# First projection group of a hybrid encoder layer: the weights' low parts on GpSimd, their products over two token blocks, a shorter norm

## The chip, the cores and the metric

The kernel runs on one core of a Trainium2 chip. The metric is the device time of one execution in microseconds (us). A core has five engines that run beside each other, each through its own instructions in order: PE (TensorE, matrix products and transposes into PSUM), DVE (VectorE) and ACT (ScalarE), which read PSUM and SBUF, POOL (GpSimd), which here works on SBUF alone, and SP, which issues DMA transfers. They wait for each other through semaphores.

## The reference

One layer: an RMSNorm of the input, one wide projection whose columns feed two token mixers (a chunkwise matrix memory and a stick-breaking attention) and two gates, a projection of each mixer, a gated sum, an output projection and the residual. Cut to what the change touches:

```python
D_MODEL = 1024; SEQ = 512; EPS = 1e-6

def rmsnorm(x, w):
    xf = x.astype(jnp.float32)
    y = xf * lax.rsqrt(jnp.mean(xf * xf, axis=-1, keepdims=True) + EPS)
    return (y * w.astype(jnp.float32)).astype(x.dtype)

h = rmsnorm(x, norm_w)
proj = jnp.einsum('bsd,de->bse', h, w_in) + b_in      # w_in: 1024 x 11272
```

The first group that the kernel computes is 512 columns of `w_in`: the queries of the first four attention heads, for all 512 tokens.

## The kernel before

**Products in three parts.** [...] A product is three matmuls into one PSUM bank: high by high, low by high, high by low. For weights the high part is a copy by ACT (`AF.Copy`) and the low part a subtraction by DVE (`split`, L96 to L98).

**The normalised input.** The 512 tokens are four blocks (tb) of 128. For a block, `x_scale` (L277) squares and sums the rows on ACT, makes the row's factor r = (mean + eps)^-0.5 with two small POOL instructions (`rstd`, L273: a scalar multiply-add and a power) and multiplies the rows by it on DVE (L290). The first block comes in two halves, with one POOL addition more (L286). `x_turn` (L292) then transposes the block on PE in two groups of four 128x128 pieces, into PSUM; DVE multiplies by the norm's weights `nw_t` and writes the high parts `hh` of a group (L302, one instruction) and its low parts `hl` (L306, four). `nw_t` itself is a PE transpose of the weights' rows and a DVE copy (L231, L232).

**The first group.** The program works through units in a hand-written order (the loop at L1226): at unit c it evacuates unit c - 1, prepares later weights, and issues the products of unit c in two halves. The first four units are the four token blocks of the first group, and each wants all eight k pieces (128 rows each) of that group's weights. So the weights of all four units (two k pieces each; L1141 to L1145 load them, the fourth into a buffer named P5) are split ahead of the loop: `first_split` (L1132) writes high parts `fh` on ACT and low parts `fl` on DVE for units 0 and 2, on POOL for units 1 and 3. `first_mm` (L1172) runs per k piece the three products in a row, into the bank `f_ps[tb]`: L1179 (hh by fh), L1180 (hl by fh), L1181 (hh by fl). A unit has two halves of four k pieces; `x_turn(c + 1)` stands between the halves of units 0 and 1, `x_turn(3)` behind unit 1. `x_scale(1)` is ahead of the loop, `x_scale(2)` and `x_scale(3)` are behind the first half of unit 0 and its `x_turn(1)`. Each engine's order is the order in which the code issues to it; no scheduler moves anything. Ahead of all this PE runs 11 matmuls on zeros (`warm`, L1155).

**Evacuation.** Unit c - 1's bank is read by DVE (L347, `qraw`) at the start of unit c. Four PSUM banks (`dps`) serve the dense products. Later weights arrive in three buffers `stg`, which units 0 to 2 hold first.

Of the kernel before, what the change touches and what calls it, by code (L numbers as in the profile page):

```python
# [8 lines left out]
F32 = mybir.dt.float32  # L9
FR = mybir.dt.float32r  # L10
BF = mybir.dt.bfloat16
AF = mybir.ActivationFunctionType
OP = mybir.AluOpType

D = 1024
T = 512
KT = 8
TB = 4
NQK = 18
EPS = 1e-6  # L20
# [15 lines left out]
def tile_hybrid_layer(  # L36
# [16 lines left out]
    nc = tc.nc  # L53
# [21 lines left out]
    def blk(tag, dt=F32, shape=(512,), name=None, p=128):  # L75

        where = mp if tag in MISC else sp
        return where.tile([p] + list(shape), dt, name=name or tag, tag=tag, bufs=BUFS[tag])

    def two(tag, dt=F32, name=None):  # L80

        t = blk(tag, dt, (2, 512), name=name)
        return t[:, 0, :], t[:, 1, :]

    def dense_ps():
        return psd.tile([128, 512], F32, name="dps", tag="dps")

    def att_ps():
        return psa.tile([128, 512], F32, name="aps", tag="aps")
# [40 lines left out]
    units = []  # L130
# [59 lines left out]
    def h_sta(k, tb):  # L190
        ts = slice(tb * 128, (tb + 1) * 128)
        return hh[:, k, ts], hl[:, k, ts]
# [27 lines left out]
    mhalf = cst.tile([128, 8], F32, name="mhalf")  # L220
# [6 lines left out]
    nw_t = cst.tile([128, 8], F32, name="nw_t")  # L227

    def norm_vec():
        vp = att_ps()  # L230
        nc.tensor.transpose(vp[:, 0:8], v_rows[0:8, :], ident[0:8, 0:8])  # L231
        nc.vector.tensor_copy(nw_t, vp[:, 0:8])  # L232

    def load_vecs():
        for j in range(4):
# [37 lines left out]
    def rstd(dst, ssq, n, eps):  # L273
        nc.gpsimd.tensor_scalar(dst, ssq, 1.0 / n, eps, op0=OP.mult, op1=OP.add)
        nc.gpsimd.tensor_tensor(dst, dst, mhalf[:, 0:dst.shape[1]], op=OP.pow)

    def x_scale(tb):  # L277
        xs = tiny.tile([128, 4], F32, name="xs", bufs=2)
        ssq, r = xs[:, 0:2], xs[:, 2:3]
        xn = x_t[tb]  # L280
        junk = blk("om", BF, (D,), name="junk")
        if tb == 0:
            for i in range(2):
                c = slice(i * D // 2, (i + 1) * D // 2)
                nc.scalar.activation(junk[:, c], xn[:, c], AF.Square, accum_out=ssq[:, i:i + 1])
            nc.gpsimd.tensor_tensor(ssq[:, 0:1], ssq[:, 0:1], ssq[:, 1:2], op=OP.add)  # L286
        else:
            nc.scalar.activation(junk, xn, AF.Square, accum_out=ssq[:, 0:1])
        rstd(r, ssq[:, 0:1], D, EPS)
        nc.vector.tensor_scalar(xn, xn, r, None, op0=OP.mult)  # L290

    def x_turn(tb):  # L292
        ts = slice(tb * 128, (tb + 1) * 128)
        xn = x_t[tb]
        for g in range(2):
            ks = slice(4 * g, 4 * g + 4)
            tp = att_ps()
            for j in range(4):
                kt = g * 4 + j
                nc.tensor.transpose(tp[:, j * 128:(j + 1) * 128], xn[:, kt * 128:(kt + 1) * 128], ident)  # L300
            dh = hh[:, ks, ts]
            nc.vector.tensor_tensor(dh, tp.rearrange("p (k t) -> p k t", k=4),  # L302
                                    nw_t[:, ks].unsqueeze(2).to_broadcast([128, 4, 128]), op=OP.mult)
            for j in range(4):
                k = 4 * g + j
                nc.vector.scalar_tensor_tensor(hl[:, k, ts], tp[:, j * 128:(j + 1) * 128], nw_t[:, k:k + 1],  # L306
                                               hh[:, k, ts].bitcast(F32), op0=OP.mult, op1=OP.subtract)
# [245 lines left out]
    def gates_fill():  # L553
        wg = blk("P5", FR, (KT, 128), name="wg")
        nc.gpsimd.memset(wg.bitcast(F32), 0.0)
        wg_t.append(wg)
# [505 lines left out]
    u = []  # L1062
# [66 lines left out]

    f_w = []  # L1130

    def first_split(i, low=None):  # L1132
        u = units[i]
        his = two("qk", FR, name="fh")
        for j in range(2):
            hi, lo = his[j], blk("y", FR, name="fl")
            nc.scalar.activation(hi, u.st[:, j, :], AF.Copy)
            (low or nc.vector).tensor_tensor(lo, u.st[:, j, :], hi.bitcast(F32), op=OP.subtract)
            f_w.append((hi, lo))

    units[0].load()  # L1141
    units[1].load()
# [12 lines left out]
    def warm(n):  # L1155
        for _ in range(n):
            nc.tensor.matmul(wp, idle[:, 0:128], idle, start=True, stop=True)

    warm(9)
    norm_vec()  # L1160
    x_scale(0)
    warm(2)
    first_split(0)
    x_turn(0)
    first_split(1, nc.gpsimd)
    x_scale(1)
    first_split(2)
    first_split(3, nc.gpsimd)

    f_ps = []  # L1170

    def first_mm(tb):  # L1172
        def mm(half):
            if half == 0:
                f_ps.append(dense_ps())
            for k in range(4 * half, 4 * half + 4):
                sh, sl = h_sta(k, tb)
                wh, wl = f_w[k]
                nc.tensor.matmul(f_ps[tb], sh, wh, start=k == 0, stop=False)  # L1179
                nc.tensor.matmul(f_ps[tb], sl, wh, start=False, stop=False)  # L1180
                nc.tensor.matmul(f_ps[tb], sh, wl, start=False, stop=k == KT - 1)  # L1181
        return mm

    for tb in range(TB):
        units[tb].mm = first_mm(tb)

    later.setdefault(3, []).append(turn_vecs)
    later.setdefault(GATES_PREP, []).append(gates_prep)
# [30 lines left out]
    def ahead(c):  # L1219
        while count["ready"] < min(N, c + AHEAD + 1):  # L1220
            fetch(count["ready"] + 1)
            units[count["ready"]].split()
            count["ready"] += 1
        fetch(c + LOADS + 1)

    for c in range(N):  # L1226
        now[0] = c
        if 0 < c < TB:
            ahead(c)
        if c and units[c - 1].slow:  # L1230
            units[c - 1].slow()
            ahead(c)
        due = later.pop(c, [])
        if c > n_proj - 9:
            ahead(c)
        if c:
            units[c - 1].evac()
        for fn in due:
            fn()
        ahead(c)  # L1240
        units[c].mm(0)
        if c < 2:
            x_turn(c + 1)
        if c == 0:
            x_scale(2)
            x_scale(3)
            gates_fill()
        for g in list(act):
            if c in REST:
                continue  # L1250
            if next(g, "end") == "end":
                act.remove(g)
        for e in list(pend):
            if c >= e[0] and e[2]():
                pend.remove(e)
                g = e[3]()
                next(g)
                act.append(g)
        units[c].mm(1)
        if c == 1:  # L1260
            x_turn(3)
# [31 lines left out]
```

## Time and profile before

| | |
|---|---|
| three runs | 692.78, 693.33, 693.89 us; median 693.33 us |
| profiled execution | 692.25 us, its span from first to last instruction 690.5 us |
| outside the span | 1.75 us |
| DVE busy | 466.4 us (68%) |
| ACT busy | 337.2 us (49%) |
| POOL busy | 118.1 us (17%) |
| granted TensorE clock, mean | 0.999 |

Of the page, the row of busy time tells which engine has no room; the view of waits tells how long an engine stood and for what; the timeline, cut to the first 32 us, gives start and length of each instruction of the first group. In a timeline row the first number is the start in us from the span's begin, the second the length, `x2` says that two instructions are merged, and what stands in brackets is idle time before it and what ended it. A PE matmul of 512 columns is shown with a length of 0.39 us, but follows its neighbour 0.23 us after that one's start.

### The profile page before, as it was taken

How to read it: one execution, taken by the hardware profiler on the slowest of the kernel's cores; microseconds unless marked ns; L12 is line 12 of the kernel's file. 1: busy time of each engine (PE TensorE's matmuls, PEld its weight loads, DVE VectorE, ACT ScalarE, POOL GpSimd, SP SyncE). 2: the span in 40 equal slices, each digit the busy share in tenths (PEclk: the TensorE clock that was granted, in tenths of full speed). 3: DMA queues.
4: the chain of work that ended last, by engine and by line, in shares of the span. 5: the costliest groups of instructions: out<-in, count | busy, mean ns of one | idle time of the engine just before them, and what ended most of it. 6: DMA issues, size and time to landing. Idle time of an engine off the chain costs nothing.

```text
span 690.5 us, 9365 instructions
## 1 busy us (share of the span) xinstructions
PE 681.7 (99%) x3150; PEld 568.2 (82%) x3150; DVE 466.4 (68%) x815; ACT 337.2 (49%) x631; POOL 118.1 (17%) x270
## 2 busy tenths in 40 slices
PE   7999999999999999999999999999999999999997
PEld 5888888888888888888888888888888888888885
DVE  6845787777997886789834648994352364445995
ACT  6235374565554653244466433447554343344451
POOL 5222032365430310000011210001112000111021
PEclk9999999999999999999999999999999999999999
DMA  7423544535553533553341343434223465599344
GB/s 249 138 92 109 155 117 121 144 89 152 146 157 102 130 106 85 124 109 92 106 110 59 106 103 90 127 89 135 71 64 90 114 189 189 140 210 207 108 90 124
DMA packets 122577, 85.27 MB, mean 123 GB/s; under 512 B 19050, under 2 KB 105988, under 8 KB 122528
## 3 DMA queue, kind: packets, MB, share of 16 engines
q1 hardware_dynamic: 119600, 77.97, 40.0%
q0 software_dynamic: 2784, 6.56, 5.1%
q8 instruction: 25, 0.41, 0.2%
q14 instruction: 24, 0.20, 0.1%
q10 hardware_dynamic: 144, 0.13, 0.1%
HBM read 66.22 MB, written 2.15 MB: 99 GB/s over the span
## 4 chain that ended last, share of the span: by engine, by line
PE 88%; issue 6%; DMA 3%; POOL 1%; DVE 1%; ACT 0%; SPq 0%; DVEq 0%; POOLq 0%
PE dps L92 25%; PE dps L93 25%; PE dps L94 25%; PE aps L93 2%; PE aps L94 2%; PE aps L92 2%; DMA xr<-in_x_dram 1%; PE dps L1181 1%; PE dps L1179 1%; PE dps L1180 1%; DMA xr<-u 1%; DMA stg<-in_w_in_dram 1%; PE aps L794 1%; PE aps L796 1%; PE aps L795 1%
## 5 line engine op out<-in xcount | busy, mean ns | idle before, releaser
L98 DVE TENSOR_TENSOR wl<-stg,wh 128x1024 fp32r<-128x1024 f32 x92 | 112.5, 1223 | 107.8 <-ACT wh L97 107.5
L92 PE MATMUL dps<-hh,wh 128*128 128x512 f32 x448 | 175.0, 391 | 0.0
L94 PE MATMUL dps<-hh,wl 128*128 128x512 f32 x448 | 174.4, 389 | 0.0
L93 PE MATMUL dps<-hl,wh 128*128 128x512 f32 x448 | 174.4, 389 | 0.0
L97 ACT ACTIVATE wh<-stg 128x1024 fp32r<-128x1024 f32 x92 | 96.8, 1052 | 65.3 <-PE dps L94 45.1
L94 PEld LDWEIGHTS dps<-hh,wl 128*128 128x128 f32 x448 | 84.1, 188 | 17.7
L93 PEld LDWEIGHTS dps<-hl,wh 128*128 128x128 f32 x448 | 84.1, 188 | 16.8
L92 PEld LDWEIGHTS dps<-hh,wh 128*128 128x128 f32 x448 | 84.2, 188 | 16.7
L92 PE MATMUL dps<-wh,hh 128*128 128x512 f32 x224 | 87.7, 392 | 0.0
L94 PE MATMUL dps<-wh,hl 128*128 128x512 f32 x224 | 87.3, 390 | 0.0
L93 PE MATMUL dps<-wl,hh 128*128 128x512 f32 x224 | 87.2, 389 | 0.0
L94 PEld LDWEIGHTS dps<-wh,hl 128*128 128x128 f32 x224 | 42.0, 188 | 9.0
L92 PEld LDWEIGHTS dps<-wh,hh 128*128 128x128 f32 x224 | 42.1, 188 | 8.3
L93 PEld LDWEIGHTS dps<-wl,hh 128*128 128x128 f32 x224 | 42.1, 188 | 8.2
L687 DVE SCALAR_TENSOR_TENSOR acc<-tmp,vec,acc 128x511 f32<-128x511 f32 (+2 forms) x48 | 36.0, 750 | 1.7
L690 ACT ACTIVATE tmp<-acc 128x512 f32<-128x512 f32 x16 | 10.1, 633 | 50.8 <-DVE acc L687 50.8
L463 POOL TENSOR_SCALAR_AFFINE_SELECT om<-om 128x128 f32<-128x128 f32 x32 | 15.4, 480 | 96.2 <-ACT om L461 96.1
L747 POOL TENSOR_SCALAR_AFFINE_SELECT w_all<-om 128x128 f32<-128x128 f32 x16 | 6.9, 465 | 142.1 <-DMA om<-rb_d 142.1
L469 DVE TENSOR_TENSOR_SCAN om<-om 128x512 f32<-128x512 f32 (+3 forms) x32 | 26.7, 834 | 5.5 <-POOL om L463 5.5
L461 ACT ACTIVATE om<-aps,rq 128x512 f32<-128x512 f32 (+3 forms) x32 | 16.8, 525 | 20.9 <-PE aps L94 20.9
L92 PE MATMUL dps<-yh,wh 128*128 128x512 f32 x64 | 24.9, 389 | 0.0
L93 PE MATMUL dps<-yl,wh 128*128 128x512 f32 x64 | 24.9, 389 | 0.0
(249 smaller groups left out, 1218.5 us busy)
## 6 DMA issues: line engine op xcount, KB each, us to landing
stg<-in_w_in_dram SPq DMA_DIRECT2D x87, 512.0 KB, 3.9
az<-ay SPq DMA_DIRECT2D x128, 40.0 KB, 2.8
stg<-in_w_proj_s_dram SPq DMA_DIRECT2D x8, 512.0 KB, 4.1
B<-in_w_out_dram SPq DMA_DIRECT2D x8, 512.0 KB, 5.8
stg<-in_w_proj_m_dram SPq DMA_DIRECT2D x8, 512.0 KB, 5.7
wl<-stg POOLq DMA_DIRECT2D x8, 512.0 KB, 5.8
tz<-ty SPq DMA_DIRECT2D x72, 32.0 KB, 1.9
brow<-in_b_in_dram SPq DMA_DIRECT2D x8, 256.0 KB, 4.4
```

The costliest lines, as they stand in the source:

```text
L92: nc.tensor.matmul(ps, ah, bh, start=first, stop=False)
L93: nc.tensor.matmul(ps, ah, bl, start=False, stop=False)
L94: nc.tensor.matmul(ps, al, bh, start=False, stop=last)
L97: nc.scalar.activation(hi, src, AF.Copy)
L98: nc.vector.tensor_tensor(lo, src, hi.bitcast(F32), op=OP.subtract)
L461: nc.scalar.activation(om[:, 0:n], zp, AF.Sigmoid, scale=rn[:, h:h + 1])
L463: nc.gpsimd.affine_select(out=om[:, ts], in_=om[:, ts], compare_op=OP.is_gt, fill=1.0, base=0, channel_multiplier=1, pattern=[[-1, 128]])
L469: nc.vector.tensor_tensor_scan(back, back, back, 1.0, op0=OP.mult, op1=OP.bypass)
L687: nc.vector.scalar_tensor_tensor(acc[:, j:], t[:, 0:T - j], cw(3 - j, ch), acc[:, j:], op0=OP.mult, op1=OP.add)
L690: nc.scalar.activation(t, acc, AF.Sigmoid)
L794: nc.tensor.matmul(nm[:, 0:258], ph, vh, start=j == 0, stop=False)
L795: nc.tensor.matmul(sum_v, ph, vl, start=False, stop=False)
```

## The change

It does four things, all ahead of or within the first four units.

1. The low parts `fl` of all eight k pieces are made by POOL, in pieces placed around the norm steps (`first_lo`); ACT's copies stay where they were.
2. Units 0 and 1 are run in another order. The products with `fl` stand behind main products (`first_main`: hh by fh, hl by fh) of later k pieces, those of k 4 to 7 of block 0 behind all main products of block 1. Two banks are then open at once, and both are evacuated at the start of unit 2. Units 2 and 3 keep their order.
3. The norm has one instruction less for the first block: r is the power -0.5 of (sum + sum + D*eps), the factor sqrt(D) goes into `nw_t`. For the other blocks POOL clears the second sum first, one instruction more.
4. `x_scale(2)` stands ahead of the loop, ahead of the last two `fl`.

```diff
-        nc.vector.tensor_copy(nw_t, vp[:, 0:8])
+        nc.vector.tensor_scalar(nw_t, vp[:, 0:8], D ** 0.5, None, op0=OP.mult)
...
-            nc.gpsimd.tensor_tensor(ssq[:, 0:1], ssq[:, 0:1], ssq[:, 1:2], op=OP.add)
         else:
+            nc.gpsimd.memset(ssq[:, 1:2], 0.0)
             nc.scalar.activation(junk, xn, AF.Square, accum_out=ssq[:, 0:1])
-        rstd(r, ssq[:, 0:1], D, EPS)
+
+        nc.gpsimd.tensor_scalar(r, ssq[:, 0:1], ssq[:, 1:2], D * EPS, op0=OP.add, op1=OP.add)
+        nc.gpsimd.tensor_tensor(r, r, mhalf[:, 0:1], op=OP.pow)
         nc.vector.tensor_scalar(xn, xn, r, None, op0=OP.mult)
...
+    def first_hi(i):
         his = two("qk", FR, name="fh")
         for j in range(2):
-            hi, lo = his[j], blk("y", FR, name="fl")
-            nc.scalar.activation(hi, u.st[:, j, :], AF.Copy)
-            (low or nc.vector).tensor_tensor(lo, u.st[:, j, :], hi.bitcast(F32), op=OP.subtract)
-            f_w.append((hi, lo))
+            nc.scalar.activation(his[j], units[i].st[:, j, :], AF.Copy)
+            f_w.append((his[j], blk("y", FR, name="fl")))
+
+    def first_lo(*ks):
+
+        for k in ks:
+            hi, lo = f_w[k]
+            nc.gpsimd.tensor_tensor(lo, units[k // 2].st[:, k % 2, :], hi.bitcast(F32), op=OP.subtract)
...
-    first_split(0)
+    first_hi(0)
     x_turn(0)
-    first_split(1, nc.gpsimd)
+    first_lo(0, 1)
+    first_hi(1)
+    first_lo(2)
     x_scale(1)
-    first_split(2)
-    first_split(3, nc.gpsimd)
+    first_lo(3)
+    first_hi(2)
+    first_hi(3)
+    first_lo(4, 5)
+    x_scale(2)
+    first_lo(6, 7)
...
+    def first_main(tb, ks):
+
+        if ks[0] == 0:
+            f_ps.append(dense_ps())
+        for k in ks:
+            sh, sl = h_sta(k, tb)
+            nc.tensor.matmul(f_ps[tb], sh, f_w[k][0], start=k == 0, stop=False)
+            nc.tensor.matmul(f_ps[tb], sl, f_w[k][0], start=False, stop=False)
+
+    def first_rest(tb, ks):
+        for k in ks:
+            nc.tensor.matmul(f_ps[tb], h_sta(k, tb)[0], f_w[k][1], start=False, stop=k == KT - 1)
...
+            if tb == 0 and half == 0:
+                first_main(0, range(4))
+                first_rest(0, range(2))
+                first_main(0, range(4, 6))
+            elif tb == 0:
+                first_rest(0, range(2, 4))
+                first_main(0, range(6, 8))
+            elif tb == 1 and half == 0:
+                first_main(1, range(8))
+            elif tb == 1:
+                first_rest(0, range(4, 8))
+                first_rest(1, range(8))
...
+    first_evacs = [units[0].evac, units[1].evac]
+    units[0].evac = lambda: None
+    units[1].evac = lambda: [fn() for fn in first_evacs]
...
         if c == 0:
-            x_scale(2)
             x_scale(3)
```

How it moves instructions is seen in each engine's order. First POOL, from the first block's norm on, before: `xs` holds a block's sums and its r (157 is block 0, 201 block 1, 258 block 2), `fl_195` and `fl_198` are the low parts of k 2 and 3, `fl_215` and `fl_218` those of k 6 and 7.

```order
L286 TENSOR_TENSOR xs_157<-xs_157 128x1
L274 TENSOR_SCALAR xs_157<-xs_157 128x1
L275 TENSOR_TENSOR xs_157<-xs_157,mhalf_91 128x1
L1138 TENSOR_TENSOR fl_195<-stg_115,fh_194 128x512
L1138 TENSOR_TENSOR fl_198<-stg_115,fh_194 128x512
L274 TENSOR_SCALAR xs_201<-xs_201 128x1
L275 TENSOR_TENSOR xs_201<-xs_201,mhalf_91 128x1
L1138 TENSOR_TENSOR fl_215<-P5_121,fh_214 128x512
L1138 TENSOR_TENSOR fl_218<-P5_121,fh_214 128x512
L274 TENSOR_SCALAR xs_258<-xs_258 128x1
L275 TENSOR_TENSOR xs_258<-xs_258,mhalf_91 128x1
```

The same engine and place of the changed kernel, behind the first block's norm: `xs_199` is now block 1, `xs_219` block 2, and `fl_168`, `170`, `195`, `197`, `209`, `211` are k 0 to 5.

```order
L1144 TENSOR_TENSOR fl_168<-stg_113,fh_166 128x512
L1144 TENSOR_TENSOR fl_170<-stg_113,fh_166 128x512
L1144 TENSOR_TENSOR fl_195<-stg_115,fh_193 128x512
L287 MEMSET xs_199 128x1
L290 TENSOR_SCALAR xs_199<-xs_199 128x1
L291 TENSOR_TENSOR xs_199<-xs_199,mhalf_91 128x1
L1144 TENSOR_TENSOR fl_197<-stg_115,fh_193 128x512
L1144 TENSOR_TENSOR fl_209<-stg_119,fh_207 128x512
L1144 TENSOR_TENSOR fl_211<-stg_119,fh_207 128x512
L287 MEMSET xs_219 128x1
L290 TENSOR_SCALAR xs_219<-xs_219 128x1
L291 TENSOR_TENSOR xs_219<-xs_219,mhalf_91 128x1
```

Block 1's factor stands behind three low parts where it stood behind two, block 2's behind six where it stood behind four. DVE before, from the scaling of block 0 (`x_80`) to the first high parts of block 1 (from `aps_238`); `x_117` is block 1:

```order
L290 TENSOR_SCALAR x_80<-x_80,xs_157 128x1024
L1138 TENSOR_TENSOR fl_168<-stg_113,fh_167 128x512
L1138 TENSOR_TENSOR fl_171<-stg_113,fh_167 128x512
L302 TENSOR_TENSOR hh_98<-aps_174,nw_t_97 128x4x128
L306 SCALAR_TENSOR_TENSOR hl_99<-aps_174,nw_t_97,hh_98 128x128 x4
L302 TENSOR_TENSOR hh_98<-aps_184,nw_t_97 128x4x128
L306 SCALAR_TENSOR_TENSOR hl_99<-aps_184,nw_t_97,hh_98 128x128 x4
L290 TENSOR_SCALAR x_117<-x_117,xs_201 128x1024
L1138 TENSOR_TENSOR fl_208<-stg_119,fh_207 128x512
L1138 TENSOR_TENSOR fl_211<-stg_119,fh_207 128x512
L302 TENSOR_TENSOR hh_98<-aps_238,nw_t_97 128x4x128
```

DVE of the changed kernel, the same place; `x_123` is block 2, and `aps_247` holds the transposes of block 1:

```order
L292 TENSOR_SCALAR x_80<-x_80,xs_157 128x1024
L304 TENSOR_TENSOR hh_98<-aps_171,nw_t_97 128x4x128
L308 SCALAR_TENSOR_TENSOR hl_99<-aps_171,nw_t_97,hh_98 128x128 x4
L304 TENSOR_TENSOR hh_98<-aps_181,nw_t_97 128x4x128
L308 SCALAR_TENSOR_TENSOR hl_99<-aps_181,nw_t_97,hh_98 128x128 x4
L292 TENSOR_SCALAR x_117<-x_117,xs_199 128x1024
L292 TENSOR_SCALAR x_123<-x_123,xs_219 128x1024
L304 TENSOR_TENSOR hh_98<-aps_247,nw_t_97 128x4x128
```

The four subtractions are gone, and the scaling of block 2 now stands ahead of block 1's high parts, where it stood behind them. PE of the changed kernel from the end of unit 0's first half to the first product of unit 1 (`dps_284`; unit 0's bank is `dps_232`); `fh_207` is k 4 and 5, `fh_212` k 6 and 7:

```order
L1190 MATMUL dps_232<-fh_207,hl_99 128x512
L302 MATMUL aps_247<-ident_86,x_117 128x128 x4
L302 MATMUL aps_257<-ident_86,x_117 128x128 x4
L1194 MATMUL dps_232<-fl_195,hh_98 128x512
L1194 MATMUL dps_232<-fl_197,hh_98 128x512
L1189 MATMUL dps_232<-fh_212,hh_98 128x512
L1190 MATMUL dps_232<-fh_212,hl_99 128x512
L1189 MATMUL dps_232<-fh_212,hh_98 128x512
L1190 MATMUL dps_232<-fh_212,hl_99 128x512
L1189 MATMUL dps_284<-fh_166,hh_98 128x512
```

Behind block 1's transposes stand 6 matmuls of unit 0, where 12 stood, and the first product of unit 1, which takes block 1's high parts, comes next.

More of the change, by code (lines that the diff above doesn't have):

```diff
@@ L1130, in tile_hybrid_layer @@
     f_w = []
-    def first_split(i, low=None):
-        u = units[i]
+    def first_hi(i):
         his = two("qk", FR, name="fh")
         for j in range(2):
-            hi, lo = his[j], blk("y", FR, name="fl")
-            nc.scalar.activation(hi, u.st[:, j, :], AF.Copy)
-            (low or nc.vector).tensor_tensor(lo, u.st[:, j, :], hi.bitcast(F32), op=OP.subtract)
-            f_w.append((hi, lo))
+            nc.scalar.activation(his[j], units[i].st[:, j, :], AF.Copy)
[4 more added lines that the diff above has]
+            nc.gpsimd.tensor_tensor(lo, units[k // 2].st[:, k % 2, :], hi.bitcast(F32), op=OP.subtract)
     units[0].load()
@@ L1162, in tile_hybrid_layer @@
     warm(2)
-    first_split(0)
+    first_hi(0)
     x_turn(0)
-    first_split(1, nc.gpsimd)
+    first_lo(0, 1)
+    first_hi(1)
+    first_lo(2)
     x_scale(1)
-    first_split(2)
-    first_split(3, nc.gpsimd)
-    f_ps = []
+    first_lo(3)
[4 more added lines that the diff above has]
+    first_lo(6, 7)
+    f_ps = []
+    def first_main(tb, ks):
[8 more added lines that the diff above has]
+            nc.tensor.matmul(f_ps[tb], h_sta(k, tb)[0], f_w[k][1], start=False, stop=k == KT - 1)
     def first_mm(tb):
         def mm(half):
[L1174 to L1181, printed above, removed]
+            if tb == 0 and half == 0:
[10 more added lines that the diff above has]
+                first_rest(1, range(8))
+            else:
+                for k in range(4 * half, 4 * half + 4):
+                    first_main(tb, [k])
+                    first_rest(tb, [k])
         return mm
```

## The prediction

> **What bounds the kernel now.** I read the page's busy row first, then what PE waits for, then whether anything behind the first group gives PE a pause, then the first 32 us in order of time.
>
> ```profile
> PE 681.7 (99%) x3150; PEld 568.2 (82%) x3150; DVE 466.4 (68%) x815; ACT 337.2 (49%) x631; POOL 118.1 (17%) x270
> PE dps L1157 <- DVE idle L1152: 1.5, 1, 1.5
> PE dps L1179 <- ACT fh L1137: 1.3, 1, 1.3
> PE aps L300 <- DVE x L290: 0.8, 1, 0.8
> PE dps L1181 <- DVE fl L1138: 0.7, 1, 0.7
> PE   7999999999999999999999999999999999999997
> ```
>
> PE is the bound. The four waits are all that the view lists for it (total, times, longest), and the last row, the span in 40 slices with PE's busy share in tenths, places them: only the first slice, 17 us long, and the last fall short of 9. The change leaves the number of matmuls as it is. So its worth is read from one instant: **when PE starts the first product of unit 2**, from where on both programs run the same products. A shift there goes through to the end.
>
> ```profile
> 6.96 1.10 PE L300 MATMUL aps<-ident,x 128*128 128x128 f32 x8
> 9.40 0.47 PE L1179 MATMUL dps<-fh,hh 128*128 128x512 f32 x1 [1.34 <-ACT fh L1137]
> 9.70 0.49 PE L1180 MATMUL dps<-fh,hl 128*128 128x512 f32 x1
> 10.03 0.39 PE L1181 MATMUL dps<-fl,hh 128*128 128x512 f32 x1
> ...
> 20.87 0.39 PE L1181 MATMUL dps<-fl,hh 128*128 128x512 f32 x1
> 21.10 1.03 PE L300 MATMUL aps<-ident,x 128*128 128x128 f32 x8
> 21.89 0.48 PE L1179 MATMUL dps<-fh,hh 128*128 128x512 f32 x1
> 22.21 0.40 PE L1180 MATMUL dps<-fh,hl 128*128 128x512 f32 x1
> ...
> 25.51 0.48 PE L1179 MATMUL dps<-fh,hh 128*128 128x512 f32 x1
> ```
>
> Unit 2 starts at **25.51**. A matmul follows the one before after 0.23 us (20.87 to 21.10), the first behind a block's transposes takes 0.32 (21.89 to 22.21), and the eight transposes take 0.79 (21.10 to 21.89).
>
> **What the change takes away.** The norm of block 0 first.
>
> ```profile
> 4.94 0.19 POOL L286 TENSOR_TENSOR xs<-xs 128x1 f32<-128x1 f32 x1 [3.49 <-ACT junk L285]
> 5.22 0.19 POOL L274 TENSOR_SCALAR xs<-xs 128x1 f32<-128x1 f32 x1
> 5.49 0.56 POOL L275 TENSOR_TENSOR xs<-xs,mhalf 128x1 f32<-128x1 f32 x1
> 5.96 0.17 DVE L232 COPY nw_t<-aps 128x8 f32<-128x8 f32 x1 [4.50 <-PE aps L231]
> 6.15 0.76 DVE L290 TENSOR_SCALAR x<-x,xs 128x1024 f32<-128x1024 f32 x1
> ```
>
> One step of 0.28 us (4.94 to 5.22) goes, so r is there at 5.78 in place of 6.05. But DVE, in order, makes `nw_t` ahead of the scaling, until 6.13, and that waits for PE. The scaling stays at 6.15: worth **0**. The multiply that replaces the copy, 8 columns wide, is costed as the copy's 0.17; at most it takes the 0.76 of a multiply over 1024 columns, 0.6 more, which the wait found below would hide.
>
> Without the two subtractions DVE reaches block 0's high parts earlier.
>
> ```profile
> 7.35 1.29 DVE L1138 TENSOR_TENSOR fl<-stg,fh 128x512 fp32r<-128x512 f32 x2 [0.45 <-ACT fh L1137]
> 8.56 0.69 DVE L302 TENSOR_TENSOR hh<-aps,nw_t 128x512 fp32r<-128x512 f32 x1
> ```
>
> Half of block 0's eight transposes (6.96, 1.10 for all) are done near 7.6, so `hh` starts at 7.65 in place of 8.56 and PE's first product at about 8.5 in place of 9.40. That 0.9 us counts only if nothing stops PE later.
>
> **What it adds: POOL's queue.** Block 1's and block 2's factors now stand behind three and six low parts.
>
> ```profile
> 6.69 1.15 ACT L1137 ACTIVATE fh<-stg 128x512 fp32r<-128x512 f32 x2 [1.83 <-DMA stg<-in_w_in_dram]
> 8.23 1.15 ACT L1137 ACTIVATE fh<-stg 128x512 fp32r<-128x512 f32 x2 [0.39 <-DMA stg<-in_w_in_dram]
> 10.72 1.16 ACT L1137 ACTIVATE fh<-stg 128x512 fp32r<-128x512 f32 x2
> 13.36 1.06 ACT L288 ACTIVATE junk<-x 128x1024 bf16<-128x1024 f32 x1 [0.21 <-DMA x<-in_x_dram]
> 8.93 1.29 POOL L1138 TENSOR_TENSOR fl<-stg,fh 128x512 fp32r<-128x512 f32 x1 [2.88 <-ACT fh L1137]
> 10.18 1.29 POOL L1138 TENSOR_TENSOR fl<-stg,fh 128x512 fp32r<-128x512 f32 x1
> 11.55 0.19 POOL L274 TENSOR_SCALAR xs<-xs 128x1 f32<-128x1 f32 x1
> 11.83 0.56 POOL L275 TENSOR_TENSOR xs<-xs,mhalf 128x1 f32<-128x1 f32 x1
> L462 POOL MEMSET om<- 128x1 f32 x32 | 3.1, 96 | 0.0
> ```
>
> ACT's order does not change. POOL's k 2 started 0.70 behind the start of ACT's copy (8.23 to 8.93), so k 0 starts at 6.69 + 0.70 = 7.39. A low part takes 1.29 us, and the next starts 1.25 behind it (8.93 to 10.18). Three end at 7.39 + 2.50 + 1.29 = 11.18. A clear (0.1), the addition and the power (from the start at 11.55 to 12.39: 0.84, with 0.08 ahead) bring **r of block 1 at 12.19**, where it was 12.39: a gain of 0.2 us, no more. ACT's k 4 and k 5, 0.7 and 1.3 us behind 10.72, are there before POOL wants them.
>
> Then come the low parts of k 3, 4 and 5. At 1.25 each from 12.14 they end at 15.93, and with the same 1.05 us **r of block 2 comes at 16.98 at the earliest**. The squares of block 2 (13.36 and 1.06 us, and a short read of the sum) are long there. Before, block 2's scaling ran behind block 1's high parts; now DVE must run it ahead of them. So block 1's high parts, which started at 16.48, cannot start before 17.0 + 0.67 = 17.67 (DVE's next instruction started 0.67 behind the scaling's start, 12.42 to 13.09, next fence).
>
> **The collision.** What DVE and POOL do to each other shows where both work on SBUF:
>
> ```profile
> 12.42 0.76 DVE L290 TENSOR_SCALAR x<-x,xs 128x1024 f32<-128x1024 f32 x1 [0.25 <-POOL xs L275]
> 12.71 1.61 POOL L1138 TENSOR_TENSOR fl<-P,fh 128x512 fp32r<-128x512 f32 x1 [0.33 <-ACT fh L1137]
> 13.09 1.77 DVE L1138 TENSOR_TENSOR fl<-stg,fh 128x512 fp32r<-128x512 f32 x1
> 14.27 1.74 POOL L1138 TENSOR_TENSOR fl<-P,fh 128x512 fp32r<-128x512 f32 x1
> 16.48 0.68 DVE L302 TENSOR_TENSOR hh<-aps,nw_t 128x512 fp32r<-128x512 f32 x1
> ```
>
> POOL's 1.29 became 1.61 behind DVE's scaling: it ends 1.29 after 13.03, just when the scaling ends. DVE's subtraction, 0.65 as one of two at 7.35, took 1.77 behind that. They take turns, each waiting for the other's whole instruction. While DVE reads PSUM (from 8.56 on) POOL keeps 1.29.
>
> In the changed kernel each scaling is released by a power, and POOL's next low part stands right behind the power. POOL's next instruction starts 0.05 before the recorded end of the one ahead (14.27, where 12.71 + 1.61 is 14.32); DVE started 0.03 behind the power's end (12.42, against 12.39). I let **POOL win**, by that 0.08 us. Then k 3 runs 12.14 to 13.43, block 1's scaling ends at 14.0, k 4 runs from 13.85 and k 5 ends at 16.39; r of block 2 is there at 17.43. k 6 runs first, until 18.67; the scaling, effective from 18.5, gives way to block 1's high parts at 19.22; these end at 19.9 and PE starts unit 1 at **20.05** (0.15 behind, as 9.40 stands behind 8.56 + 0.69). If DVE wins both, k 3 to 5 start after 12.83, r of block 2 comes at 17.66 and PE starts at **19.2**. With no collision at all: 17.67 + 0.68 + 0.15 = **18.5**.
>
> [...]
>
> **Is PE really empty until then?** Behind block 1's transposes (14.05) stand 6 matmuls of unit 0, the last starting near 16.1. Before, 12 stood there. So PE waits some 3.6 us at the head of unit 1. From there to unit 2 stand 28 matmuls (16 main, 12 with `fl`) and 16 transposes: 28 x 0.2275 + 2 x (0.79 + 0.09) + 0.17 for the slow start (9.40 to 10.03 in place of 2 x 0.23) = 8.3 us. DVE's `hh` and `hl` of block 1 come at the pace of block 0's, behind which PE went from 9.40 on without a listed wait for them, and k 6 and 7 of `fl` end at 20.4, long before they are read. Unit 2 starts at 28.35 (POOL wins), 27.5 (DVE wins) or 26.8 (no collision): **+2.84, +2.0 or +1.3 us** against 25.51.
>
> **What costs nothing.** SP's loads into the three `stg` buffers wait for POOL now:
>
> ```profile
> 17.57 1.41 SPq L117 DMA_DIRECT2D stg<-in_w_in_dram x3
> ```
>
> It comes to them at 17.57, and by the forecast k 5 is done at 16.4; the cover is about a microsecond. The two evacuations at unit 2 delay only norms of queries that are used far later, and the fourth bank is still that of the zeros. Nobody waits there.
>
> **The rivals.**
>
> *DVE wins the race* (+2.0). [...]
>
> *No collision* (+1.3): against it speak the rows above.
>
> *POOL is quicker alone* and the kernel is not slower. All four low parts were timed with DVE at work. The forecast needs 1.25 us each; at 1.03 us (six of them 1.3 us shorter) the loss is gone, and from there block 2's squares (14.5) take over: r at 15.4, unit 2 at 25.25, -0.25 us, 693.1 at best. Against it: 1.29 us twice, beside DVE instructions of quite different lengths, looks like POOL's own rate.
>
> *PE falls back to its slow rate* in the long wait:
>
> ```profile
> 1.51 4.21 PE L1157 MATMUL dps<-idle 128*128 128x512 f32 x9 [1.51 <-DVE idle L1152]
> ```
>
> Nine matmuls on zeros took 4.21 at the start, 0.47 each, against 0.23 later. If PE runs so from 1.51 to the transposes at 6.96, 5.45 us, and does it again, that is 11.6 matmuls with 0.24 more each, +2.8 on top of the forecast: 699.0. The trace has no wait of this length, so it doesn't tell. [...]
>
> *The change doesn't do what it says*: the order of instructions shows that it does.
>
> **How the numbers follow.** The sum is against the profiled execution (690.5 us span, 1.75 around it, 692.25), which is 1.08 below the median of the runs; the shift is added to the median. POOL wins 0.43, 696.2; DVE wins 0.25, 695.3; no collision 0.12, 694.6; slow rate 0.07, 699.0; POOL quicker 0.08, 693.1; anything else 0.05. The range 694.2 to 697.4 holds the first three and leaves out the others. A measurement of this kernel can tell about 0.2%, 1.4 us: slower takes the first two, half of the third and the slow rate, 0.81; same the other half and the quicker POOL, 0.14; to faster I give the unnamed rest, 0.05.
>
> **What would show it.** A wait of PE of over 2 us ahead of block 1's first product, ended by `hh`; DVE idle until about 17; block 2's scaling right behind, or one low part behind, POOL's second power; first product near 8.5; unit 2 near 28. It is wrong if low parts take about 1.0 us, or if unit 1 starts before 17.2.

## The result and the profile after

| | before | changed |
|---|---|---|
| runs | 692.25 to 693.89 us (6) | 697.29 to 700.04 us (6) |
| median | 692.94 us | 698.25 us |
| ratio, 95% interval | 1 | 1.0076 (1.0061 to 1.0092) |
| profiled execution, its span | 692.25 us, 690.5 us | 700.04 us, 698.3 us |
| mean granted clock | 0.999 | 0.995 |

The changed kernel is slower by 5.3 us in the medians, by 7.8 us between the two profiled executions; that of the changed kernel is the slowest of its six, that of before the fastest of its six. The forecast was slower by 2.84 us with a range up to 697.4: the direction is right, the time lies outside.

PE's waits in the changed kernel (total in us, times, longest; L1189 is hh by fh, L302 a block's transposes, L575 the gates' products, L94 a product of the later units):

```profile
PE dps L1189 <- DVE hh L304: 3.4, 1, 3.4
PE aps L302 <- DVE x L292: 2.2, 2, 1.3
PE dps L1162 <- DVE idle L1157: 1.5, 1, 1.5
PE aps L575 <- DVE wg L565: 0.9, 1, 0.9
PE dps L94 <- DMA wl<-stg: 0.5, 1, 0.5
PE dps L1189 <- ACT fh L1137: 0.4, 1, 0.4
```

The 3.4 us are the forecast wait for block 1's high parts. New beside it are 0.9 us at the gates' products, which come behind unit 3, and 0.5 us for a transfer near the end (at 649.6 us). POOL and DVE of the same kernel in order of time (L1144 is a low part, L291 the power, L292 the scaling, L304 the high parts):

```profile
11.48 0.58 POOL L291 TENSOR_TENSOR xs<-xs,mhalf 128x1 f32<-128x1 f32 x1
12.02 4.22 POOL L1144 TENSOR_TENSOR fl<-stg,fh 128x512 fp32r<-128x512 f32 x3
...
16.76 0.57 POOL L291 TENSOR_TENSOR xs<-xs,mhalf 128x1 f32<-128x1 f32 x1
17.30 2.93 POOL L1144 TENSOR_TENSOR fl<-P,fh 128x512 fp32r<-128x512 f32 x2
```

```profile
12.09 1.76 DVE L292 TENSOR_SCALAR x<-x,xs 128x1024 f32<-128x1024 f32 x1 [0.41 <-POOL xs L291]
17.36 1.75 DVE L292 TENSOR_SCALAR x<-x,xs 128x1024 f32<-128x1024 f32 x1 [3.51 <-POOL xs L291]
19.03 0.68 DVE L304 TENSOR_TENSOR hh<-aps,nw_t 128x512 fp32r<-128x512 f32 x1
```

Block 2's factor is there at 17.33 (16.76 + 0.57). Both scalings start 0.06 to 0.07 us behind POOL's next low part and take 1.75 us in place of 0.75. PE then, from unit 0's last product on:

```profile
16.01 0.39 PE L1190 MATMUL dps<-fh,hl 128*128 128x512 f32 x1
19.76 0.79 PE L1189 MATMUL dps<-fh,hh 128*128 128x512 f32 x1 [3.36 <-DVE hh L304]
20.35 0.63 PE L1190 MATMUL dps<-fh,hl 128*128 128x512 f32 x1
20.78 0.63 PE L1189 MATMUL dps<-fh,hh 128*128 128x512 f32 x1
...
25.47 0.60 PE L1190 MATMUL dps<-fh,hl 128*128 128x512 f32 x1
25.90 0.40 PE L1189 MATMUL dps<-fh,hh 128*128 128x512 f32 x1
26.14 0.39 PE L1190 MATMUL dps<-fh,hl 128*128 128x512 f32 x1
...
30.81 0.48 PE L1189 MATMUL dps<-fh,hh 128*128 128x512 f32 x1
```

Unit 1 starts at 19.76, and its products follow each other after 0.43 us (20.35 to 20.78; the first after 0.59) until 25.9, then after 0.23. Unit 2 starts at 30.81, 5.30 us behind before. The windows of 2 us show why (behind the busy times of PE, PE's weight loads, DVE, ACT and POOL, the third last column is the granted clock, then come the share and the rate of the DMA):

```profile
16.00:18.00 2.00, 0.40 (x2) 0.00 (x0) 0.64 (x1) 0.00 (x0) 1.82 (x5) 1.00 0.06 14
18.00:20.00 2.00, 0.24 (x1) 0.24 (x1) 1.96 (x3) 0.00 (x0) 2.00 (x2) 0.77 0.72 118
20.00:22.00 2.00, 2.00 (x5) 1.57 (x6) 1.96 (x7) 0.00 (x0) 1.82 (x5) 0.50 0.92 279
22.00:24.00 2.00, 2.00 (x6) 1.55 (x5) 1.29 (x4) 1.03 (x1) 0.21 (x1) 0.50 1.04 400
24.00:26.00 2.00, 2.00 (x6) 1.52 (x6) 0.00 (x0) 0.03 (x1) 0.00 (x0) 0.52 0.31 121
26.00:28.00 2.00, 2.00 (x15) 1.73 (x14) 0.96 (x3) 0.00 (x0) 0.00 (x0) 1.00 0.04 8
```

While PE waited its clock was halved (0.77 over 18 to 20 us), and it stayed so for nearly 7 us: the rival to which the forecast gave 0.07. All six executions of the changed kernel show a mean clock of 0.995 to 0.998. The mean alone doesn't say that the clock fell at this place: in the comparisons below 12 of 48 executions of before show 0.995 to 0.998 too, and in before's trace it falls in the last microsecond (0.77 over 689 to 690 us, 0.50 behind that), where PE has nothing left to do (its last product starts at 685.8).

### The profile page after: what moved, and what is told of

The parts are those of the page before. It is cut to its first block, busy times and chain, and to the rows that moved or that the text cites. A ratio compares the mean times of both kernels' runs of the same rounds, so it can differ in the third digit from the quotient of the medians.

```text
span 698.3 us, 9369 instructions
## 1 busy us (share of the span) xinstructions
PE 684.5 (98%) x3150; PEld 569.8 (82%) x3150; DVE 464.1 (66%) x811; ACT 337.1 (48%) x631; POOL 123.7 (18%) x276
## 4 chain that ended last, share of the span: by engine, by line
PE 79%; issue 10%; DMA 6%; DVE 2%; POOL 2%; ACT 1%; SPq 0%; DVEq 0%; POOLq 0%
PE dps L92 23%; PE dps L94 23%; PE dps L93 23%; PE aps L93 2%; PE aps L94 2%; PE aps L92 2%; DMA wl<-stg 2%; DMA stg<-in_w_proj_m_dram 1%; POOL fl L1144 1%; DMA xr<-u 1%; DMA xr<-in_x_dram 1%; PE aps L796 1%; PE aps L798 1%; PE aps L797 1%; POOL xr L1062 1%
## 5 line engine op out<-in xcount | busy, mean ns | idle before, releaser
L94 PE MATMUL dps<-hh,wl 128*128 128x512 f32 x448 | 174.4, 389 | 0.0
L94 PEld LDWEIGHTS dps<-hh,wl 128*128 128x128 f32 x448 | 84.1, 188 | 17.8
L94 PE MATMUL dps<-wh,hl 128*128 128x512 f32 x224 | 87.3, 390 | 0.0
L94 PEld LDWEIGHTS dps<-wh,hl 128*128 128x128 f32 x224 | 42.1, 188 | 8.9
L94 PE MATMUL dps<-yh,wl 128*128 128x512 f32 x64 | 25.0, 391 | 0.5 <-DMA wl<-stg 0.5
```

The source lines that it names most:

```text
L94: nc.tensor.matmul(ps, al, bh, start=False, stop=last)
```

## The experiments

The theory: three costs add up, the wait at unit 1 made by the order (block 2's scaling ahead of block 1's high parts, behind six low parts), the half clock behind that wait, and the gates' wait. Against it stand that the low parts on POOL are the wait wherever the scaling stands, and that the slow products have another cause than the wait. Ratios are to runs of before on the same chip.

**e1, fill.** The wait stays, but PE is busy in it. The 14 matmuls work on zeros and add nothing to the output.

```diff
                 first_rest(0, range(2, 4))
                 first_main(0, range(6, 8))
+                warm(14)
```

> The changed kernel with 14 more matmuls on zeros behind unit 0's last product; they write a bank that nobody reads. Theory clock (the long wait of PE at unit 1 lets its clock fall to half): the granted clock stays at 1.0 over 18 to 26 us, the first 16 products of unit 1 follow each other after 0.23 us in place of 0.43, unit 1 still starts near 19.8 and unit 2 near 28.0; the time falls by 2 to 3 us against the changed kernel, to about 695.5. Rival (the slow rate has another cause, such as the transfers or the DVE and GpSimd work at that place): unit 1 keeps 0.43 us per product and the time stays at 698 or rises by what the added matmuls take.

Measured 695.82 us, ratio 1.0036 (1.0024 to 1.0048), against 1.0076. PE of this run:

```profile
16.57 3.34 PE L1162 MATMUL dps<-idle 128*128 128x512 f32 x14
20.12 0.50 PE L1189 MATMUL dps<-fh,hh 128*128 128x512 f32 x1 [0.21 <-DVE hh L304]
...
21.08 0.39 PE L1190 MATMUL dps<-fh,hl 128*128 128x512 f32 x1
21.31 0.40 PE L1189 MATMUL dps<-fh,hh 128*128 128x512 f32 x1
...
28.47 0.48 PE L1189 MATMUL dps<-fh,hh 128*128 128x512 f32 x1
```

Unit 1 starts no earlier than in the changed kernel, its products follow after 0.23 us and unit 2 starts 2.34 us earlier. Transfers and the other engines' work are the same there (the DMA's share over 20 to 22 and 22 to 24 us is 0.92 and 1.04 in the changed kernel, 0.99 and 1.04 here), so the slow rate came from PE's idleness. The difference of the two ratios puts its price at about 2.8 us (0.0040 x 693), with the intervals of both 1.4 to 4.1.

**e2, mul_back.** DVE's scaling of block 2 alone goes back behind block 1's high and low parts.

```diff
-    def x_scale(tb):
+    x_mul = {}
+
+    def x_scale(tb, mul=True):
...
-        nc.vector.tensor_scalar(xn, xn, r, None, op0=OP.mult)
+        x_mul[tb] = lambda: nc.vector.tensor_scalar(xn, xn, r, None, op0=OP.mult)
+        if mul:
+            x_mul[tb]()
...
-    x_scale(2)
+    x_scale(2, False)
     first_lo(6, 7)
...
         if c == 0:
+            x_mul[2]()
             x_scale(3)
```

> The changed kernel with only DVE's scaling of block 2 moved back behind the high and low parts of block 1; GpSimd and ACT keep their order. Theory order (the scaling's place on DVE, behind six low parts of GpSimd, makes the wait): PE's wait at unit 1 falls from 3.4 us to under 0.5, there is no slow clock, unit 2 starts at 24.3 to 25, ahead of the 25.5 of before. Theory evacuation (two evacuations at once delay ACT's squares, and with them the weights of the gates): PE then waits some 1 to 3 us ahead of the gates' products, so that the time is 692 to 694.5, not clearly faster than before. Rival (GpSimd's low parts themselves are the wait): unit 1 still waits over 2 us, for low parts or for block 1's factor.

Measured 696.62 us, ratio 1.0050 (1.0038 to 1.0062), above the 692 to 694.5 expected. The waits and the clock of this run:

```profile
PE aps L579 <- DVE wg L569: 3.0, 1, 3.0
PE dps L1166 <- DVE idle L1161: 1.5, 1, 1.5
PE aps L306 <- DVE x L294: 1.5, 2, 1.0
PE dps L1193 <- DVE hh L308: 0.4, 1, 0.4
```

```profile
36.00:38.00 2.00, 0.00 (x0) 0.00 (x0) 2.00 (x6) 0.28 (x2) 1.00 (x2) 1.00 0.00 0
38.00:40.00 2.00, 1.26 (x5) 1.03 (x6) 1.13 (x5) 1.79 (x11) 0.42 (x2) 0.87 0.00 0
40.00:42.00 2.00, 2.00 (x6) 1.61 (x5) 0.00 (x0) 1.14 (x6) 1.67 (x4) 0.50 0.00 0
```

The long wait at unit 1 is gone and with it the rival that blames the low parts; unit 2 starts at 24.03, 1.48 us ahead of before. But PE reaches the gates' products earlier and waits 3.0 us for their weights, and there the clock falls to half as well. That was expected as a wait; the half clock behind it was not. Together they gave away more than the lead.

**e3, scale_back.** Block 2's whole norm goes back to its old place.

```diff
-    x_scale(2)
     first_lo(6, 7)
...
         if c == 0:
+            x_scale(2)
             x_scale(3)
```

> The changed kernel with the whole norm of block 2 (squares, GpSimd's steps, the scaling) put back to its old place, behind all eight low parts. Theory order: no long wait at unit 1, but block 2's factor comes at about 20.2, so its transposes wait about 1 us and unit 2 starts near 25.5; time 692.5 to 695. Rival as for the run before: unit 1 still waits over 2 us.

Measured 696.31 us (694.35 to 697.96), ratio 1.0045 (1.0028 to 1.0062), above the range expected. Unit 1 does not wait long and block 2's transposes wait 0.65 us, where about 1 us was expected; but the gates' wait is 2.25 us (36.86 to 39.11), and the clock fell to half here too:

```profile
38.00:40.00 2.00, 0.89 (x3) 0.72 (x4) 1.49 (x8) 1.74 (x9) 0.13 (x1) 0.83 0.00 0
40.00:42.00 2.00, 2.00 (x6) 1.56 (x5) 0.00 (x0) 1.48 (x8) 1.58 (x5) 0.50 0.00 0
```

The one execution of the six whose mean clock is 1.0 is the fastest, 694.35 us.

**e4, norm_only.** The kernel before with the shorter norm and nothing else (the lines of the change in `norm_vec` and `x_scale`).

> The kernel before with nothing but the shorter norm. Theory (DVE makes the norm's weights ahead of the scaling, which hides the step saved): block 0's scaling starts within 0.1 us of 6.15 and the time is within 0.1% of before. Rival: the scaling starts 0.28 us earlier and the time falls by 0.2 to 0.3 us, or the clear that is added on GpSimd for the other blocks makes it later by 0.1 to 0.3 us.

Measured 692.84 us, ratio 1.0000 (0.9991 to 1.0008). DVE makes the norm's weights until 6.08, the scaling starts at 6.09:

```profile
5.03 0.31 POOL L289 TENSOR_SCALAR xs<-xs 128x1 f32<-128x1 f32 x1 [3.59 <-ACT junk L285]
5.42 0.57 POOL L290 TENSOR_TENSOR xs<-xs,mhalf 128x1 f32<-128x1 f32 x1
5.91 0.17 DVE L232 TENSOR_SCALAR nw_t<-aps 128x8 f32<-128x8 f32 x1 [4.46 <-PE aps L231]
6.09 0.75 DVE L291 TENSOR_SCALAR x<-x,xs 128x1024 f32<-128x1024 f32 x1
```

The shorter norm is worth nothing here. Of the 0.28 us saved, 0.12 are lost in it, too: the addition of two columns takes 0.31 us, where the multiply-add with constants took 0.19.

**e5, back_gates.** e2, with the gates' small weights made a unit earlier on DVE.

```diff
-GATES_PREP, GATES_START, GATES_SCAN = 3, 4, 35
+GATES_PREP, GATES_START, GATES_SCAN = 2, 4, 35
```

> Block 2's scaling moved back as in the run mul_back, and the gates' small weights (DVE, four instructions) made one unit earlier, behind the two evacuations and ahead of unit 5's low parts. Theory (mul_back lost its lead only by the gates' wait of 3.0 us and by the half clock behind it): that wait goes to under 0.3 us, the clock stays at 1.0, unit 2 starts near 24.1 where it was 25.5; the time is 1.0 to 1.6 us below before. Rival (the late squares of two blocks hold up something else): PE waits 1 us or more at unit 4 or 5 and the time is not below before.

Measured 691.88 us, ratio 0.9973 (0.9962 to 0.9985): 1.9 us below before (1.0 to 2.6). The gates' wait is not listed any more. Its profiled execution is the slowest of seven (693.54 us): POOL's first low part waited for ACT's first copy until 8.03 (6.90 in e2), and block 1's transposes waited 1.67 us until 14.76 (13.64 in e2). They took 1.37 us (0.85 in e2), and the products behind them followed each other after 0.43 us until 18.41, from 18.69 on after 0.23; by this spacing the half rate lasted from about 15.1 to 18.5, an estimate. So the clock did not stay at 1.0 there, as had been expected (its mean is 0.997), and unit 2 started at 26.78 and not near 24.1. The other six lie at 691.09 to 692.23.

**e6, gates_early.** The changed kernel with only that one number changed.

> The changed kernel with only the gates' small weights made one unit earlier. Theory: the wait ahead of the gates' products (0.95 us) goes and nothing else moves: unit 1 still waits 3.4 us, half clock behind it, time about 0.9 us below the changed kernel, 697 to 697.6. Rival (the wait is hidden by something else that is late as well): no change.

Measured 697.77 us, ratio 1.0051 (1.0037 to 1.0064). The gates' wait is gone, the wait of 3.36 us at unit 1 and the half clock remain (products 0.43 us apart from 20.82 on, mean clock 0.996). The ratio's interval overlaps that of the change; that this alone is faster is not shown by the times, but the wait's disappearance is by the trace. PE of this run:

```profile
19.84 0.49 PE L1189 MATMUL dps<-fh,hh 128*128 128x512 f32 x1 [3.36 <-DVE hh L304]
...
23.38 0.53 PE L1189 MATMUL dps<-fh,hh 128*128 128x512 f32 x1
23.74 0.40 PE L1190 MATMUL dps<-fh,hl 128*128 128x512 f32 x1
...
29.77 0.48 PE L1189 MATMUL dps<-fh,hh 128*128 128x512 f32 x1
```

The wait is as long and ends at the same place as in the changed kernel, but the slow products end at 23.7 and not at 25.9, and unit 2 starts 1.04 us earlier than there (29.77 against 30.81). So the price of the half clock differs between executions whose wait is the same.

**e7, fill_guard.** e1, with a small clear on POOL behind the two powers, so that DVE comes first.

```diff
+    gap = cst.tile([128, 128], F32, name="gap")
...
         nc.gpsimd.tensor_tensor(r, r, mhalf[:, 0:1], op=OP.pow)
+        if tb in (1, 2):
+            nc.gpsimd.memset(gap, 0.0)
```

> The run fill with a clear of 128x128 on GpSimd (0.2 us) behind the powers of blocks 1 and 2, so that DVE's scaling comes ahead of the next low part. Theory (the collision is a lock that the first holds): both scalings take 0.75 us in place of 1.75, unit 1 starts 0.5 to 0.9 us earlier (near 19.4), the time falls by as much to about 695.2. [...]

Measured 695.25 us, ratio 1.0023 (1.0014 to 1.0031); the interval overlaps that of e1, so the gain is read from the trace. DVE and POOL of this run:

```profile
18.12 0.75 DVE L295 TENSOR_SCALAR x<-x,xs 128x1024 f32<-128x1024 f32 x1 [4.76 <-POOL xs L292]
18.79 0.68 DVE L307 TENSOR_TENSOR hh<-aps,nw_t 128x512 fp32r<-128x512 f32 x1
```

```profile
17.51 0.57 POOL L292 TENSOR_TENSOR xs<-xs,mhalf 128x1 f32<-128x1 f32 x1
18.03 0.20 POOL L294 MEMSET gap<- 128x128 f32 x1
18.20 3.06 POOL L1147 TENSOR_TENSOR fl<-P,fh 128x512 fp32r<-128x512 f32 x2
```

The scaling starts 0.08 us ahead of the low part and takes 0.75 us; block 1's, at 12.60, takes 0.76. The low part beside each takes 1.81 to 1.82 us, where those of the changed kernel that start ahead of the scaling take 1.26 to 1.28. Unit 1 starts at 19.52 where it was 20.12 in e1. In these rows and in those of the changed kernel the one that starts first keeps its length (0.75 to 0.76 us, 1.26 to 1.28 us), and the other takes longer (1.81 to 1.82 us, 1.75 to 1.76 us).

**e8, back_gates_guard.** e5 with the same clears.

> The run back_gates with the same clears behind the two powers. Theory lock: block 1's transposes start near 12.7 in place of 13.6, but unit 0's second half then waits for the low part of k 3, so unit 2 starts 0.3 to 0.9 us earlier still, near 23.5, and the time is 1.5 to 2.2 us below before. Rival: the low part of k 3 comes so late that nothing is won against back_gates.

Measured 691.64 us, ratio 0.9972 (0.9961 to 0.9983). Block 1's transposes start at 13.15, unit 2 at 24.42, not at 23.5: the twelve products with low parts ahead of it take 3.38 us (2.98 in e2), block 3's transposes now wait 0.19 us for their scaling, and near the end PE waits 1.0 us for a transfer. The time, 1.9 us below before, lies in the range expected, but nothing is measurably won against e5.

**e9, fill_gates.** e1 and e6 together, so that only the wait itself is left.

> The changed kernel with both the 14 matmuls on zeros in the wait at unit 1 and the gates' small weights one unit earlier; what is left is the wait itself. Theory (the loss is a sum of three: the wait that the forecast named, the half clock behind it, the gates' wait): PE lists no wait at the gates, the clock stays at 1.0, unit 2 starts near 28.4, and the time is 0.9 us below the run fill, a ratio to before of 1.002 to 1.003. Rival (a further cost outside these): the ratio stays at 1.0036 or above.

Measured 694.70 us, ratio 1.0027 (1.0017 to 1.0038). PE lists neither a wait at the gates nor one over 1.6 us, and unit 2 starts here:

```profile
28.15 0.48 PE L1189 MATMUL dps<-fh,hh 128*128 128x512 f32 x1
```

That is 2.64 us behind before, where the forecast had 2.84; the times say 1.9 us (1.2 to 2.6). How the 5.3 us divide can't be told from the times: by way of e1 the ratios fall by 2.8 us for the clock, 0.6 for the gates and 1.9 for the wait, by way of e6 by 1.7 for the gates, 1.7 for the clock and 1.9 for the wait. Either row adds up to the whole by the way it is made, and the steps are about as wide as their intervals. The instants in the traces say more:

- the wait at unit 1: 2.64 us (e9) to 2.96 (e1), as unit 2's start against before;
- the half clock: 1.6 us (29.77 in e6 against 28.15) or 2.7 us (30.81 in the changed kernel against 28.15);
- the gates' wait: 1.2 us. The first product behind the gates starts at 47.16, where it was 40.64, so 5.30 us at unit 2 have become 6.52.

## Why the prediction was wrong

- **PE is the bound, and a shift at unit 2 goes through:** right, with additions. The 5.30 us at unit 2 are 6.5 behind the gates' wait, stay so until the wait for a transfer near the end, and are 7.3 behind it; the last transfer of `xr` took 6.45 us where it took 5.92, which makes 7.8 us of span.
- **The norm is worth 0:** right (e4). The scaling itself stood at 6.57 in the profiled execution in place of 6.15, as half of the input had landed later, so PE's first product came at 8.91 and not near 8.5 (8.40 in e2).
- **POOL's queue:** right to 0.1 us, in part by luck. Block 2's factor came at 17.33, forecast 17.43. The first low part began 0.58 us earlier than forecast (6.81 in place of 7.39, its weights had landed earlier), but took 1.64 us behind block 0's scaling, a collision that the forecast left out, and each addition took 0.31 us in place of 0.19.
- **The collision:** POOL won both, by 0.06 to 0.07 us, as forecast, and e7 shows what that costs a scaling: 1.75 us against 0.75.
- **PE's wait:** 3.36 us, forecast some 3.6; unit 1 at 19.76, forecast 20.05. By the traces this wait alone costs about what was forecast (e9: unit 2 at 28.15, e1: 28.47, forecast 28.35); by e9's times it is less, 1.9 us with an interval that ends at 2.6, below the 2.84.
- **The step that failed: 28 x 0.2275 for the products of unit 1.** The first 14 were followed after 0.43 us (the first after 0.59): they took 6.14 us in place of some 3.4, and unit 2 came 2.75 us later than 19.76 + 8.3 = 28.06. With PE kept busy in the wait, the 8.3 us hold (e1: 20.12 to 28.47). The rival had the mechanism and a price of 2.8 us. That the price fits the trace so well is luck: the rival took 0.24 us more for each product over 5.45 us, the trace shows 0.20 more over 6.8 us, and e6, behind the same wait, 1.6 us in all. How long the half rate lasted in the other five executions of the changed kernel is not known. What was wrong was the chance of 0.07, an estimate of mine with no run behind it. The wait was 3.36 us in the trace and the clock fell; it fell behind 2.25 us in e3 and behind 1.67 us in e5. The trace of before could not have told: its waits behind the warm-up are at most 1.34 us, and none was followed by products at 0.43 us.
- **"Nobody waits there" for the two evacuations:** wrong, 0.95 us as listed, 1.2 us in PE's instants. ACT squares both blocks behind each other, eight squares from 36.03 on (before, four from 31.20 on), ahead of unit 5's high parts; DVE waits for those (40.46) and stands ahead of the gates' small weights:

```profile
40.46 1.22 DVE L98 TENSOR_TENSOR wl<-stg,wh 128x1024 fp32r<-128x1024 f32 x1 [3.86 <-ACT wh L97]
41.60 0.68 DVE L349 TENSOR_TENSOR qraw<-dps,brow 128x512 f32<-128x512 f32 x1
...
42.56 0.17 DVE L564 CAST wg<-gst 128x32 fp32r<-128x32 f32 x1
```

I had asked who reads the evacuated blocks, and not what else stands behind ACT's squares in DVE's queue. With the two terms the sum is 2.84 + 2.75 + 1.2 = 6.8 us, against 6.5 us in the trace behind the gates; with e6's 1.6 us for the clock it is 5.6, against 5.3 us in the medians.
- **The transfer waited for near the end (0.5 us, 1.0 us in e8)** was not forecast. Of the eight transfers of its kind (L126) the slowest took 9.6 us in the changed kernel and 7.6 us in before, which lists no such wait, as the other eight runs list none. Why it was slow stays open.

## What to carry to other kernels

A wait on a PE that was busy throughout is to be priced with the slow rate that may follow it: here the clock fell behind five waits of 1.67 to 3.36 us, and behind the two of 3.36 us that cost another 1.6 to 2.75 us. Where an instruction is moved ahead in an engine's order, ask for the latest input that it brings with it: one scaling of 0.75 us, put ahead of block 1's high and low parts, tied block 1 to block 2's chain. The intended gain was there (unit 2 about 1.5 us earlier in e2) and could be had, 1.9 us below before in e5, once both stalls that the change made were taken away.

## What was not expected of the hardware

- The clock fell behind waits of 3.36 us (changed kernel, e6), 3.04 us (e2), 2.25 us (e3) and 1.67 us (e5), and not behind waits of 1.6 us (e9), 1.67 us (e4) and 1.71 us (e1), where the mean clock was 1.0. In e3 it fell at about 39.3, when the wait had ended (39.11) and PE was at work again. So the length of the wait alone doesn't tell: behind 1.67 us PE ran at half rate in e5 and at the full one in e4. The half rate lasted 3.4 us in e2 and e3 by the clock, 3.3 to 3.4 us in e5 and e6 by an estimate from the products' spacing, and 6.8 us in the changed kernel, twice that.
- The slow stretch of 6.8 us began at 19.1, with PE still waiting until 19.76; the four of 3.4 us began 0.2 to 0.7 us behind the end of the wait. Whether that decides between the two lengths, five falls don't show.
- The granted clock reads 1.00 over the first matmuls on zeros although they follow each other after 0.43 us: at the start of the span the spacing tells the rate, the clock column doesn't. The traces hold no clock record ahead of 6.9 us (before) and 5.4 us (changed kernel).
- POOL's addition with a second column as operand takes 0.31 us, the one with constants alone 0.19.
